# Rotary positions loaded into the table rows and the tables computed there; value stores issued by ScalarE

## The chip, the cores and the metric

The kernel runs on one core of a Trainium2 chip. The metric is the device time of one execution in microseconds (us). The engines are TensorE (PE; its weight loads are a row of their own, PEld), VectorE (DVE), ScalarE (ACT), GpSimd (POOL) and SyncE (SP), which here only issues transfers (DMAs). Each engine works through its own instructions strictly in order and waits on semaphores for what others produce.

## What is computed

One decoder layer on a sequence of 2048 tokens, model width 1024, float32. Cut to what matters here:

```python
mod = silu(c) @ w_ada + b_ada;  shift, scale, gate = split(mod, 3)
h = rms_norm(x, norm_pre) * (1 + scale) + shift
xa, ga, q, k, v, gb = split(h @ w_in)             # six groups of 512 columns
ang = positions[:, None] * 10000 ** (-arange(32) / 32)
cos, sin = cos(ang), sin(ang)                     # one table for all 8 heads
q, k = rotary(q, cos, sin), rotary(k, cos, sin)   # x1*cos - x2*sin, x2*cos + x1*sin
ya = rms_norm(rg_lru(conv(xa)) * silu(ga))
yb = rms_norm(dilated_attention(q, k, v) * silu(gb))
out = x + gate * rms_norm(concat(ya, yb) @ w_out, norm_post)
```

## The kernel before, in words

The first phase (to about 650 us of the span) makes h and all projections; attention follows, then the output projection. The change touches the first phase alone.

The sequence is cut into four chunks c of 512 tokens, done in two halves (chunks 0 and 1, then 2 and 3). Float32 products are split in high and low parts, three matmuls each. In a half the order of the program is: q and k of the first four heads for both chunks (`qk`, L376), recurrent blocks (`rec`, which calls `conv`, `ga`, `lru`), q and k of the other heads, more recurrent blocks, the values (`v`, L398) and the gate of attention (`gb`, L408). `load(c)` (L1007) loads a chunk of x, normalises it, and for chunks 2 and 3 makes the rotary table; `prep(c)` transposes it on PE (L298) and makes the high and low parts of h, `hh` on ACT (L308) and `hl` on DVE or POOL (L311, L313). In the first half `prep(1)` stands behind q and k of chunk 0, `load(2)` behind the k of the second four heads, `prep(2)` and `load(3)` behind the gate of chunk 0. The table of chunk 0 (`trig(0)`) is called ahead of `prep_h` of chunk 0, that of chunk 1 just ahead of `prep(1)`.

`trig(c)` (L238) takes a scratch buffer from `turn()`, which hands out two buffers, `half_t` and `rot_t`, in turn. The same two are the workspace of every `qk` and, in the first half, of `gb`; each is stored to DRAM from there. `trig` loads the 512 positions of the chunk to all 128 partitions of the scratch buffer (L243), converts them to float, multiplies by the frequencies, takes off multiples of two pi (DVE, L245 to L251), takes two sines and an absolute value on ACT (L253 to L256), and writes cosine and sine to rows of `cos_t` (DVE, L258 to L260). `cos_t` has four rows of 512: cosine and sine of even chunks, then of odd chunks.

`v` evacuates each tile of values from PSUM on ACT (L404) into `vr`, of which there are two buffers, and stores it to DRAM through SP's queue (L406). SP's queue also carries the weight loads (`wst`, three buffers that the loads of the gate's weights, `wgate`, L206, share; L327), the loads of x (L269) and the stores of q, k, y and gb (L395, L501, L420).

The order of instructions in this phase is not written by hand. A planner orders the instructions of each engine, and the transfers of each queue, by the order of the program and its own estimates of durations; work whose inputs it expects to be ready goes into idle time ahead of work that comes earlier in the program. On the chip this order is then fixed. The attention phase has its order written out by hand.

The DMAs that SP issues are not ordered by data alone: SP issues them one after the other, and an issue that waits holds all behind it.

Of the kernel before, what the change touches and what calls it, by code (L numbers as in the profile page):

```python
# [9 lines left out]
I32 = mybir.dt.int32  # L10
AF = mybir.ActivationFunctionType
ALU = mybir.AluOpType
# [4 lines left out]
P = 128  # L17
# [5 lines left out]
CH = 512  # L23
# [27 lines left out]
INV_TWO_PI = 1.0 / (2.0 * math.pi)  # L51
MAGIC = 12582912.0


class Layer:
# [179 lines left out]
        return self.turns[0]  # L235


    def trig(self, c):  # L238
        nc = self.nc
        v = nc.vector  # L240
        rot = self.turn()
        pi = rot[:, 0, :].bitcast(I32)
        nc.sync.dma_start(pi, self.io["positions"][:, c * CH:(c + 1) * CH].to_broadcast([P, CH]))  # L243
        a = rot[:, 1, :]
        v.tensor_copy(a, pi)  # L245
        v.tensor_scalar(a, a, self.freq, None, ALU.mult)
        n = rot[:, 2, :]
        v.tensor_scalar(n, a, INV_TWO_PI, MAGIC, ALU.mult, ALU.add)
        v.tensor_scalar(n, n, MAGIC, None, ALU.subtract)
        for part in (TWO_PI_1, TWO_PI_2, TWO_PI_3):  # L250
            v.scalar_tensor_tensor(a, n, -part, a, ALU.mult, ALU.add)  # L251
        s = rot[:, 2, :]
        nc.scalar.activation(s, a, AF.Sin, scale=0.5)  # L253
        nc.scalar.activation(a, a, AF.Abs)
        ch = rot[:, 3, :]
        nc.scalar.activation(ch, a, AF.Sin, scale=-0.5, bias=self.halfpi)  # L256
        cos, sin = (self.cos_t[:, 2 * (c % 2) + n, :] for n in range(2))
        v.tensor_mul(cos, s, s)  # L258
        v.tensor_scalar(cos, cos, -2.0, 1.0, ALU.mult, ALU.add)
        v.scalar_tensor_tensor(sin, s, 2.0, ch, ALU.mult, ALU.mult)  # L260
        return cos, sin


# [134 lines left out]
    def v(self, rw, ps, h, w, quad, c):  # L398

        nc = self.nc  # L400
        for t in range(4):
            o = self.tmajor(ps, w, h, t, "pv")
            vr = rw.tile([P, 4, DH], F32, name="vr", bufs=2)
            nc.scalar.activation(vr, o[:, 0:256].rearrange("p (h d) -> p h d", d=DH), AF.Copy, scale=0.5)  # L404
            r0 = c * CH + t * P
            nc.sync.dma_start(self.v_s[r0:r0 + P, 4 * quad:4 * quad + 4, :], vr)  # L406

    def gb(self, wst, ps, h, w, half, c):  # L408

# [547 lines left out]
    def run(self, out):  # L957
        tc, nc = self.tc, self.nc
        self.wst_bufs = 3
        with ExitStack() as top:  # L960
            def pool(stack, name, bufs=1, **kw):
                return stack.enter_context(tc.tile_pool(name=name, bufs=bufs, **kw))
# [30 lines left out]
            with ExitStack() as p1:  # L993
                psx = pool(p1, "psx", space=PSUM)
                rw = pool(p1, "rw")
                wpb = pool(p1, "wpb")
                recb = pool(p1, "recb")
                h0p = pool(p1, "h0p")
                ps = Banks((psm, 2), (psx, 4))
                hs, self.cs = {}, {}  # L1000

                def slot(c):
                    return (h1p, "s1") if c % 2 else (h0p, "s0")

                xs = {}

                def load(c):  # L1007
                    xs[c] = self.load_x(c)
                    self.normalise(rw, ps, xs[c], first=c < 2)
                    if c > 1:  # L1010
                        self.cs[c] = self.trig(c)

                def prep(c):
                    hs[c] = self.prep_h(*slot(c), c, lambda k: self.transpose_x(ps, xs[c], k), c == 1)

                with tc.tile_pool(name="ld", bufs=1) as ld:
                    x0 = []
                    self.constants(const, ld, ps, lambda: x0.extend(self.load_x(0)))
                    self.normalise(rw, ps, x0, first=True)
                    raw = []  # L1020
                    for k in range(KC):
                        rp, tag = (recb, ("xr", "xc", "xh", "xl", "ga", "a", "m")[k]) if k < 7 else (reca, "xc")
                        raw.append(rp.tile([P, CH], F32, name=f"raw{k}", tag=tag))
                        pt = self.transpose_x(ps, x0, k)
                        nc.scalar.copy(raw[k], pt)
                    ws = [h1p.tile([P, 4, 2, 512], F32, name="wada", tag=t) for t in ("s1h", "s1l")]
                    self.ada_half(ws, reca, "ri", ps, ld, 0)
                    wq = self.weights(wpa, wst, OQ, rotary=True, early=True)
                    self.ada_half(ws, recb, "ri", ps, ld, 1)
                    wk = self.weights(wpb, wst, OK_, rotary=True, early=True)  # L1030
                    self.cs[0] = self.trig(0)
                    hs[0] = self.prep_h(*slot(0), 0, lambda k: raw[k], True)
                    load(1)
                    self.gate_steps = self.ada_gate(wst, ps, ld)
                    for half in range(2):
                        c0, c1 = 2 * half, 2 * half + 1

                        def rec(j):
                            w = self.weights(wpa, wst, OXA + P * j, col2=OGA + P * j)
                            us = []  # L1040
                            for c, rp in ((c0, reca), (c1, recb)):
                                us.append(self.conv(rp, ps, hs[c], w, 0, j, c))
                                self.ga(ps, hs[c], w, 1, us[-1])
                            self.defer(3, lambda: self.lru(ps, us))

                        def values(q):
                            w = self.weights(wpb, wst, OV + 256 * q)
                            for c in (c0, c1):
                                self.v(rw, ps, hs[c], w, q, c)

                        if half:
                            wq = self.weights(wpa, wst, OQ, rotary=True)
                            wk = self.weights(wpb, wst, OK_, rotary=True)
                        for c in (c0, c1):
                            self.qk(ps, hs[c], wq, "q", 0, c)
                            self.qk(ps, hs[c], wk, "k", 0, c)
                            if c == c0:
                                if c1 == 1:
                                    self.cs[1] = self.trig(1)
                                prep(c1)  # L1060
                        if half == 0:
                            self.softplus(ld)
                            self.gate_weights(gwp, reca)
                        rec(0)
                        w = self.weights(wpb, wst, OQ + 256, rotary=True)
                        for c in (c0, c1):
                            self.qk(ps, hs[c], w, "q", 1, c)
                        rec(1)
                        w = self.weights(wpb, wst, OK_ + 256, rotary=True)
                        for c in (c0, c1):  # L1070
                            self.qk(ps, hs[c], w, "k", 1, c)
                        if half == 0:
                            load(2)
                        rec(2)
                        values(0)
                        rec(3)
                        values(1)
                        wb = [self.weights(wp, wst, OGB + 256 * q) for q, wp in enumerate((wpa, wpb))]
                        for c in (c0, c1):
                            for q in range(2):  # L1080
                                self.gb(wst, ps, hs[c], wb[q], q, c)
                            if c == 0:
                                prep(2)
                                load(3)
                    whole(self.gate_steps)
                    self.tick(6)
# [74 lines left out]
def whole(steps):  # L1161

    while True:
        try:
            next(steps)
        except StopIteration as e:
            return e.value
# [67 lines left out]
```

## Time and profile before

| | before |
|---|---|
| median of three runs | 1184.37 us (1180.71 to 1185.92) |
| the profiled execution | 1180.56 us, its span 1178.8 us |
| PE busy | 1096.3 us (93%) |
| DVE busy | 758.4 us (64%) |
| ACT busy | 612.6 us (52%) |
| POOL busy | 457.3 us (39%) |
| mean granted TensorE clock | 0.965 of full speed |

The page also cuts the span in 40 slices of 29.5 us; each digit is the busy share of a slice in tenths (9 is 90% or more), PEclk the granted clock:

```profile
PE   5868999869989999999999999999999998999996
DVE  4766497677555645879565266687597783355556
ACT  5544353447547223654545377767678674223332
PEclk9988999999999999999999999989999989999998
```

The first phase is the first 22 slices. PE is below 9 in slices 0, 1, 2 and 3, in slice 8 (236 to 265 us) and in slice 11 (324 to 354 us).

### The profile page before, as it was taken

The numbers are of one execution on the slowest core, as the hardware profiler recorded it, in microseconds if no ns is written. First come the engines' busy times: TensorE is split into PE (matmuls) and PEld (weight loads), VectorE is DVE, ScalarE is ACT, GpSimd is POOL, SyncE is SP. The second block draws the span as 40 slices with busy tenths as digits, with TensorE's granted clock in tenths as the row PEclk, the third lists the DMA queues.
The fourth block names the chain that finished last, engine by engine and source line by source line (L and its number), as shares of the span: only waits on it lengthen the run. The fifth ranks groups of instructions, "written<-read, shape, count | busy, mean of one in ns | idle before, by whom it ended". The sixth has DMA issues, their size and how long they took to land.

```text
span 1178.8 us, 18472 instructions
## 1 busy us (share of the span) xinstructions
PE 1096.3 (93%) x6645; PEld 899.0 (76%) x6645; DVE 758.4 (64%) x1655; ACT 612.6 (52%) x1512; POOL 457.3 (39%) x297
## 2 busy tenths in 40 slices
PE   5868999869989999999999999999999998999996
PEld 2546888768967778888898888878777876778885
DVE  4766497677555645879565266687597783355556
ACT  5544353447547223654545377767678674223332
POOL 1434434234143553436234170083361563742222
PEclk9988999999999999999999999989999989999998
DMA  9533335152253344427222724858659447976654
GB/s 338 191 116 131 116 119 169 60 180 90 85 147 125 110 141 135 124 91 196 82 90 77 227 77 98 179 135 221 164 124 236 127 146 147 269 231 215 186 152 143
DMA packets 164859, 176.49 MB, mean 150 GB/s; under 512 B 25168, under 2 KB 119840, under 8 KB 164768
## 3 DMA queue, kind: packets, MB, share of 16 engines
q1 hardware_dynamic: 164768, 175.32, 51.9%
q8 instruction: 52, 0.85, 0.3%
q14 instruction: 39, 0.32, 0.1%
HBM read 124.49 MB, written 50.79 MB: 149 GB/s over the span
## 4 chain that ended last, share of the span: by engine, by line
PE 52%; DMA 18%; DVE 12%; POOL 7%; issue 5%; ACT 4%; SPq 2%; DVEq 0%; POOLq 0%; ACTq 0%
PE sp L665 5%; DMA st_s<-stat 3%; PE pt L688 3%; DMA wgate<-in_w_ada 3%; DMA W<-f_s 2%; PE pvo L705 2%; PE pv L369 2%; PE pv L370 2%; PE pv L371 2%; PE pmixa L909 2%; POOL W L805 2%; PE pmixb L927 2%; PE pmixa L907 2%; PE pgb L358 2%; PE pgb L357 2%
## 5 line engine op out<-in xcount | busy, mean ns | idle before, releaser
L344 POOL TENSOR_TENSOR wl<-wst,wh 128x1024 fp32r<-128x1024 f32 (+2 forms) x72 | 138.5, 1945 | 203.1 <-ACT wh L342 203.1
L670 DVE CUSTOM_DVE_ANT_0 pm<-sp,table 128x256 f32<-128x256 f32 (+1 forms) x384 | 119.2, 360 | 48.3 <-PE sp L665 42.9
L665 PE MATMUL sp<-kh,qs 64*128 64x256 f32 (+1 forms) x768 | 131.9, 388 | 8.9 <-DVE S L670 5.2
L805 POOL TENSOR_TENSOR W<-W,o 128x512 f32<-128x512 f32 x48 | 60.7, 1294 | 151.0 <-DMA W<-f_s 151.0
L665 PEld LDWEIGHTS sp<-kh,qs 64*128 64x128 f32 x768 | 100.8, 274 | 24.0 <-issue 12.4
L688 PE MATMUL pt<-table,pm 128*128 128x128 f32 x600 | 88.8, 294 | 2.7 <-ACT pT L693 1.5
L705 PE MATMUL pvo<-pT,vt 128*64 128x128 f32 (+1 forms) x1072 | 87.6, 306 | 0.0
L342 ACT CAST wh<-wst 128x1024 fp32r<-128x1024 f32 (+2 forms) x72 | 51.8, 761 | 56.3 <-DMA wst<-in_w_in 26.6
L688 PEld LDWEIGHTS pt<-table,pm 128*128 128x128 f32 x600 | 69.4, 148 | 15.1 <-issue 3.0
L369 PE MATMUL pv<-wh,hh 128*128 128x256 f32 x256 | 72.8, 284 | 7.6 <-ACT vr L404 4.4
L705 PEld LDWEIGHTS pvo<-pT,vt 128*64 128x64 f32 x1072 | 63.4, 144 | 19.2 <-issue 14.4
L370 PE MATMUL pv<-wl,hh 128*128 128x256 f32 x256 | 72.7, 284 | 3.6 <-POOL wl L344 3.6
L952 POOL TENSOR_TENSOR mix<-mix,xt 128x1024 f32<-128x1024 f32 x15 | 36.6, 2441 | 100.1 <-DVE mix L951 60.1
L665 PE MATMUL sp<-kl,qs 64*128 64x256 f32 (+1 forms) x384 | 75.4, 366 | 0.0
L678 ACT ACTIVATE pm<-pm,stat 128x256 f32<-128x256 f32 (+1 forms) x128 | 60.2, 474 | 25.5 <-DVE stat L670 25.5
L371 PE MATMUL pv<-wh,hl 128*128 128x256 f32 x256 | 72.3, 282 | 0.0
L678 ACT ACTIVATE pm<-pm,turn 128x256 f32<-128x256 f32 (+1 forms) x128 | 62.8, 495 | 16.3 <-DVE turn L670 16.3
L357 PE MATMUL pa<-hl,wh 128*128 128x512 f32 x128 | 52.7, 412 | 17.0 <-DVE hl L313 14.7
L691 DVE COPY pT<-pt 128x512 f32<-128x512 f32 (+1 forms) x96 | 63.7, 679 | 0.8 <-PE pt L688 0.5
L665 PEld LDWEIGHTS sp<-kl,qs 64*128 64x128 f32 x384 | 57.8, 277 | 0.0
L437 DVE SCALAR_TENSOR_TENSOR xc<-xr,cols,xc 128x512 f32<-128x512 f32 x48 | 55.5, 1156 | 0.8
L369 PEld LDWEIGHTS pv<-wh,hh 128*128 128x128 f32 x256 | 49.0, 191 | 8.8 <-ACT vr L404 5.1
(275 smaller groups left out, 3131.8 us busy)
## 6 DMA issues: line engine op xcount, KB each, us to landing
wst<-in_w_in SPq DMA_DIRECT2D x32, 512.0 KB
W<-f_s SPq DMA_DIRECT2D x32, 384.0 KB
x_t<-in_x SPq DMA_DIRECT2D x16, 512.0 KB
wada<-in_w_ada SPq DMA_DIRECT2D x16, 512.0 KB
wst<-in_w_in SPq DMA_DIRECT2D x32, 256.0 KB
vt<-v_s SPq DMA_DIRECT2D x32, 256.0 KB
yat<-y_s SPq DMA_DIRECT2D x32, 256.0 KB
yb_s<-yb SPq DMA_DIRECT2D x16, 512.0 KB
```

The lines of the kernel that those rows point to most:

```text
L344: nc.gpsimd.tensor_tensor(lo, i, hi.bitcast(F32), ALU.subtract)
L357: nc.tensor.matmul(o, lhsT=wh[:, k, sl], rhs=hl[:, k, :], start=False, stop=False)
L369: nc.tensor.matmul(o[:, 0:256], lhsT=hh[:, k, sl], rhs=wh[:, k, :], start=k == 0, stop=False)
L370: nc.tensor.matmul(o[:, 0:256], lhsT=hh[:, k, sl], rhs=wl[:, k, :], start=False, stop=False)
L371: nc.tensor.matmul(o[:, 0:256], lhsT=hl[:, k, sl], rhs=wh[:, k, :], start=False, stop=k == KC - 1)
L665: nc.tensor.matmul(self.sp[h][:, o:o + n], lhsT=x[rows, q], rhs=y[rows, k], start=j == 0, stop=j == 2)
L670: v.tensor_tensor_reduce(out=pm[:, o:o + n], in0=sp[:, o:o + n], in1=self.mask[:, 256 - n:256], scale=-0.125, scalar=3e38, op0=ALU.add, op ...
L678: nc.scalar.activation(pm[:, o:o + n], pm[:, o:o + n], AF.Exp, bias=self.stat(ctx, s, b), scale=-1.0, accum_out=self.stat(ctx, 2 + s, b))
L688: nc.tensor.transpose(pt[:, k * P:(k + 1) * P], pm[:, k * P:(k + 1) * P], self.ident)
L691: nc.vector.tensor_copy(pT[:, 0:tot], pt[:, 0:tot])
L705: self.mark = nc.tensor.matmul(self.bank[p][64 * s:64 * s + 64, o:o + w], lhsT=ctx["vt"][p, b][:, s], rhs=ctx["pT"][:, c:c + w], start=fir ...
L805: e.tensor_tensor(W[:, p], W[:, p], self.o.pop((pr, p, n)), ALU.mult)
```

## The change

Positions no longer go through a scratch buffer. A new method loads them straight into the sine row of the chunk in `cos_t`; for chunks 0 and 1 it is called ahead of the modulation (`ada_half`), for chunks 2 and 3 where `load(c)` called `trig`. `trig` takes no turn of the two buffers: its steps run in place in the two rows of `cos_t`. It has the same number of instructions on DVE (ten) and on ACT (three); the product for the sine now comes before the two steps that turn the half-angle sine into the cosine. As `trig` takes no turn, the buffers of all later `qk` and `gb` calls alternate by themselves. In `v`, the store is issued on ACT's queue.

```diff
+    def load_positions(self, c):
+        pi = self.cos_t[:, 2 * (c % 2) + 1, :].bitcast(I32)
+        self.nc.sync.dma_start(pi, self.io["positions"][:, c * CH:(c + 1) * CH].to_broadcast([P, CH]))
+
     def trig(self, c):
...
-        rot = self.turn()
-        pi = rot[:, 0, :].bitcast(I32)
-        nc.sync.dma_start(pi, self.io["positions"][:, c * CH:(c + 1) * CH].to_broadcast([P, CH]))
-        a = rot[:, 1, :]
-        v.tensor_copy(a, pi)
...
+        cos, sin = (self.cos_t[:, 2 * (c % 2) + n, :] for n in range(2))
+        v.tensor_copy(sin, sin.bitcast(I32))
+        v.tensor_scalar(sin, sin, self.freq, None, ALU.mult)
+        v.tensor_scalar(cos, sin, INV_TWO_PI, MAGIC, ALU.mult, ALU.add)
+        v.tensor_scalar(cos, cos, MAGIC, None, ALU.subtract)
         for part in (TWO_PI_1, TWO_PI_2, TWO_PI_3):
-            v.scalar_tensor_tensor(a, n, -part, a, ALU.mult, ALU.add)
...
+            v.scalar_tensor_tensor(sin, cos, -part, sin, ALU.mult, ALU.add)
+        nc.scalar.activation(cos, sin, AF.Sin, scale=0.5)
+        nc.scalar.activation(sin, sin, AF.Abs)
+        nc.scalar.activation(sin, sin, AF.Sin, scale=-0.5, bias=self.halfpi)
+        v.scalar_tensor_tensor(sin, cos, 2.0, sin, ALU.mult, ALU.mult)
+        v.tensor_mul(cos, cos, cos)
         v.tensor_scalar(cos, cos, -2.0, 1.0, ALU.mult, ALU.add)
-        v.scalar_tensor_tensor(sin, s, 2.0, ch, ALU.mult, ALU.mult)
...
     def v(self, rw, ps, h, w, quad, c):
...
-            nc.sync.dma_start(self.v_s[r0:r0 + P, 4 * quad:4 * quad + 4, :], vr)
+            nc.scalar.dma_start(self.v_s[r0:r0 + P, 4 * quad:4 * quad + 4, :], vr)
...
                 def load(c):
...
                     if c > 1:
+                        self.load_positions(c)
+                    if c > 1:
                         self.cs[c] = self.trig(c)
...
                     ws = [h1p.tile([P, 4, 2, 512], F32, name="wada", tag=t) for t in ("s1h", "s1l")]
+                    for c in range(2):
+                        self.load_positions(c)
                     self.ada_half(ws, reca, "ri", ps, ld, 0)
```

## Rows read from the trace of the kernel before

**Rows 1.** By stretch: busy PE, PEld, DVE, ACT, POOL (instructions), granted clock, DMA share, GB/s.
```profile
0.00:25.00 25.00, 12.38 (x40) 4.50 (x41) 13.46 (x49) 13.97 (x26) 0.19 (x4) 1.00 0.94 331
50.00:80.00 30.00, 23.24 (x96) 17.07 (x96) 27.39 (x42) 18.45 (x32) 11.36 (x9) 0.89 0.28 83
80.00:110.00 30.00, 18.26 (x76) 14.60 (x75) 14.02 (x24) 10.18 (x19) 9.12 (x5) 0.77 0.31 114
210.00:260.00 50.00, 41.53 (x245) 35.98 (x245) 38.31 (x47) 24.28 (x37) 19.87 (x10) 0.99 0.37 119
260.00:300.00 40.00, 35.62 (x189) 30.91 (x188) 29.10 (x31) 24.37 (x39) 16.14 (x8) 0.88 0.31 100
335.00:365.00 30.00, 22.83 (x117) 18.60 (x116) 18.24 (x27) 16.53 (x23) 7.18 (x6) 0.89 0.34 97
400.00:450.00 50.00, 47.40 (x218) 37.82 (x217) 25.42 (x32) 16.41 (x25) 25.11 (x16) 1.00 0.41 120
560.00:640.00 80.00, 80.00 (x502) 72.01 (x501) 47.87 (x50) 46.48 (x76) 30.26 (x14) 1.00 0.25 84
```

**Rows 2.** Waits, 60 to 120 us: total us, times, longest.
```profile
DVE half_t L245 <- DMA half_t<-in_positions: 12.2, 1, 12.2
PE pa L357 <- DVE hl L313: 12.2, 2, 11.7
```

**Rows 3.** Timeline of DVE: start us, duration us, instruction, idle before it.
```profile
93.07 0.43 DVE L245 CAST half_t<-half_t 128x512 f32<-128x512 int32 x1 [12.21 <-DMA half_t<-in_positions]
93.41 0.69 DVE L313 TENSOR_TENSOR hl<-x_t,hh 128x512 fp32r<-128x512 f32 x1
```

**Rows 4.** Timeline of SP's queue, 70 to 84 us.
```profile
74.24 7.31 SPq L395 DMA_DIRECT2D k_s<-rot_t  x3
81.66 2.34 SPq L243 DMA_DIRECT2D half_t<-in_positions  x1
```

**Rows 5.** Busy time by stretch, just behind that wait.
```profile
96.00:99.00 3.00, 3.00 (x10) 2.41 (x9) 2.45 (x5) 1.44 (x2) 1.66 (x1) 0.50 0.00 0
```

**Rows 6.** DVE by line, 48 to 64 us: busy us, mean ns, idle before.
```profile
L251 DVE SCALAR_TENSOR_TENSOR rot_t<-rot_t 128x512 f32<-128x512 f32 x3 | 2.0, 678 | 0.0
L259 DVE TENSOR_SCALAR cos_t<-cos_t 128x512 f32<-128x512 f32 x1 | 1.4, 1406 | 0.0
```

**Rows 7.** Waits of PE, 48 to 80 us.
```profile
PE xT L298 <- DVE x_t L311: 3.4, 1, 3.4
```

**Rows 8.** Waits of all engines, 200 to 225 us.
```profile
POOL half_t L387 <- DVE half_t L385: 19.9, 1, 19.9
DVE rot_t L245 <- DMA rot_t<-in_positions: 10.8, 1, 10.8
```

**Rows 9.** Waits of PE, 225 to 260 us.
```profile
PE pv L370 <- POOL wl L344: 3.6, 2, 2.5
PE pv L369 <- ACT xc L435: 3.3, 1, 3.3
```

**Rows 10.** Timeline of ACT, 250 to 266 us, and of SP's queue, 246 to 262 us.
```profile
265.43 0.71 ACT L404 ACTIVATE vr<-pv 128x256 f32<-128x256 f32 x2 [6.08 <-DMA v_s<-vr]
...
260.94 0.38 SPq L327 DMA_DIRECT2D wst<-in_w_in  x1
261.41 0.56 SPq L406 DMA_DIRECT2D v_s<-vr  x1
```

**Rows 11.** Waits of all engines, 335 to 358 us.
```profile
PE xT L298 <- DVE x_t L311: 6.4, 1, 6.4
DVE half_t L245 <- DMA half_t<-in_positions: 3.9, 1, 3.9
```

**Rows 12.** The line of the value stores; waits of SP's queue, 0 to 655 us.
```profile
L406 SPq DMA_DIRECT2D v_s<-vr x32: 319/320/564, 252.3 to 625.6; - x32
...
SPq L406 <- DMA wst<-in_w_in: 3.0, 1, 3.0
```

**Rows 13.** DVE by line, 4 to 17 us.
```profile
L134 DVE TENSOR_SCALAR spacc<-spacc 128x4 f32<-128x4 f32 x7 | 1.2, 170 | 0.2
```

More of the change, by code (lines that the diff above doesn't have):

```diff
@@ L240, in trig @@
         v = nc.vector
-        rot = self.turn()
-        pi = rot[:, 0, :].bitcast(I32)
-        nc.sync.dma_start(pi, self.io["positions"][:, c * CH:(c + 1) * CH].to_broadcast([P, CH]))
-        a = rot[:, 1, :]
-        v.tensor_copy(a, pi)
[L246 to L249, printed above, removed]
-        for part in (TWO_PI_1, TWO_PI_2, TWO_PI_3):
-            v.scalar_tensor_tensor(a, n, -part, a, ALU.mult, ALU.add)
[L252 to L258, printed above, removed]
+        cos, sin = (self.cos_t[:, 2 * (c % 2) + n, :] for n in range(2))
[3 more added lines that the diff above has]
+        v.tensor_scalar(cos, cos, MAGIC, None, ALU.subtract)
+        for part in (TWO_PI_1, TWO_PI_2, TWO_PI_3):
+            v.scalar_tensor_tensor(sin, cos, -part, sin, ALU.mult, ALU.add)
[4 more added lines that the diff above has]
+        v.tensor_mul(cos, cos, cos)
         v.tensor_scalar(cos, cos, -2.0, 1.0, ALU.mult, ALU.add)
-        v.scalar_tensor_tensor(sin, s, 2.0, ch, ALU.mult, ALU.mult)
         return cos, sin
```

## The prediction, made before the changed kernel was run

> **What bounds the kernel now.** I read the busy shares first: PE is the fullest engine, and the changed lines all lie in the first phase, so the question is where PE stands idle there and who holds it. The busy time by stretch answers the first half [rows 1]: PE has no gap in long stretches such as 560 to 640 us, and loses its time in few places: 50 to 80 us (30 - 23.24 = 6.8 us idle), 80 to 110 (11.7), 210 to 260 (8.5), 260 to 300 (4.4) and 335 to 365 (7.2), 38.6 us in all. Each but the third also drags the granted clock down, to a mean of 0.77 to 0.89; behind the longest wait PE is fully busy at a granted clock of 0.50, the lower of its two levels (1.2 of 2.4 GHz) [rows 5]. Then the waits say who held it. In all five places a line of the change is in it.
>
> The largest place shows the pattern. SP issues the positions of chunk 1 at 81.66 us, behind the four stores of k [rows 4]; they land 11.4 us later, since DVE's first step of the table starts at 93.07 [rows 3]. DVE waits 12.2 us for them, PE 11.7 us [rows 2], though PE needs nothing of that table yet: it needs `hl`, and L313 stands behind L245 in DVE's order and starts as soon as L245 is through [rows 3]. So the loss is not the work of the table but the place of a waiting instruction in an in-order queue.
>
> **The change part by part.** All sums are against the profiled execution, 1180.56 us (span 1178.8 and 1.8 around it).
>
> *Chunk 1 (80 to 110 us).* The load moves from 81.66 us to the front of SP's queue, so L245 has nothing to wait for wherever the planner puts it. That takes 11.7 us off PE [rows 2], and the low clock with it: a mean of 0.77 over 30 us is 0.23 / 0.5 x 30 = 13.8 us at the lower level, of which about 9 fell in the idle time and 5 were work at half speed, 2.5 us lost. Next in line is `prep(1)` itself: DVE still has three pairs of L311 and L313 to do, at 0.7 to 0.8 us each, and PE may wait for the last; I keep 1.7 us for that. Gain 12.5 us, between 8 and 14.
>
> *The table of chunk 0 (50 to 80 us).* DVE is busy 27.4 of 30 us here [rows 1], and the chain of waits runs through it. Ten instructions of the table, 0.4 to 1.4 us each (the three of L251 make 2.0 us, L259 1.4 [rows 6]), are 7.1 us of it. With positions there from the start they can run in DVE's idle time before 50 us (25 - 13.46 = 11.5 us in the first 25 [rows 1]). That the planner does such things is seen: the softplus steps, which the program calls behind q and k of chunk 0, ran among the first instructions, at 4 to 17 us [rows 13]. PE would have x of chunk 1 earlier, on which it waits 3.4 us [rows 7] of its 6.8, with another 1.7 us at the lower clock (0.11 / 0.5 x 30 = 6.6 us, about half of it work). The new order of the sine and cosine products makes the cosine wait for one ACT step and one product more, about 1.5 us, which is hidden if the table is early. Bounds: -4 (the moved steps get in the way further up) and +8.5; I take +4.5, the middle, nearest to the wait of 3.4 us and its clock.
>
> *The start.* Two loads of 0.26 MB now stand ahead of the modulation's weights, in a stretch with a DMA share of 0.94 at 331 GB/s [rows 1]: 0.52 MB / 331 GB/s = 1.6 us later for the weights. Chunk 0's load was already in the busy stretch, and PE has slack of under a microsecond there: -1 us, between 0 and -1.6, plus what the moved DVE steps cost (above).
>
> *Chunk 2 (210 to 260 us).* DVE waits 10.8 us for positions, POOL 19.9 us for DVE behind that [rows 8], and PE then waits 3.6 us for POOL's `wl` and 3.3 for ACT's `xc`, both late from that [rows 9]: 6.9 us. The load no longer waits for the stores of the scratch buffer, but for DVE's last reading of the sine row, a few microseconds earlier, and is issued ahead of the stores of k rather than behind. The landing itself stays, so I leave DVE 3 of its 10.8 us, and PE 3 / 10.8 of its loss, 1.9 us. Gain 5, between 0 and 7.
>
> *The value stores (255 to 275 us).* ACT waits 6.1 us to reuse `vr` [rows 10]: the store of its last content was issued only at 261.41, behind a weight load that SP had waited to issue till 260.94. PE waits 4.4 us of the 4.4 idle in 260 to 300, and 5 us of work there ran at the lower clock (0.12 / 0.5 x 40 = 9.6 us, less 4.4 idle), 2.6 us. On ACT's queue the store is issued as soon as the tile is written. The price is 32 issues of 0.32 us [rows 12], 10.2 us of ACT; in the second half they lie beside a PE that is full while ACT is busy 46 of 80 us [rows 1], so they cost nothing there, and in the first half ACT has 15.6 of 40 us free. If that cover were gone, all 10.2 us would count. Gain 6 of 7, between -3 and 7.
>
> A rule speaks against this part. The Trainium skill (DMA: Bandwidth & Descriptors, "Issuing engines are not separate DMA queues") says that transfers from any issuing engine share the same 16 DMA engines, and that issuing from several only saves issue time. By that rule 0.32 us per store would be all, and the sum would end 6 us later. The trace differs in what an issue can cost: here SP's queue held a store behind another transfer's wait, and ACT's reader for 6.1 us [rows 10].
>
> *Chunk 3 (335 to 365 us).* DVE waits 3.9 us for positions, which waited for a store of gb out of `half_t`, and PE 6.4 us behind it [rows 11]; 0.11 / 0.5 x 30 = 6.6 us at the lower clock, half of it work, 1.6 us lost. The sine row of chunk 1 is free 100 us earlier, so the table can be made long before. Of 7.2 + 1.6 us I take 7.5, between 4 and 9. Of ACT's table loads I expect as many as before, since the three activations stay.
>
> *What stays.* Stretches without such a wait keep small ones (2.6 us in 400 to 450 [rows 1]); the new order will have its own. I take off 3 us. Attention and the output projection start earlier by the sum and do not change.
>
> Sum: 12.5 + 4.5 - 1 + 5 + 6 + 7.5 - 3 = 31.5 us. 1180.6 - 31.5 = 1149.1 in the profiled execution. The median of the runs is 3.8 us above it, so I predict 1153 us.
>
> **The rivals.**
>
> *Positions still late.* The loads of chunks 2 and 3 may land behind stores of k again, as in rows 4, with DVE's L245 placed too early by a planner whose estimate was wrong by 10 us before. For: rows 8 show that error. Against: the sine row is free before the stores are ready. Then chunk 2 gives nothing and chunk 3 half: 1153 + 5 + 3.5 = 1161.5, say 1162. 18%.
>
> *The moved tables get in the way.* Two tables of 7.1 us are 14.2 us of DVE against 11.5 us idle in the first 25, and the modulation that all waits for runs on DVE there. Then 50 to 80 us loses 4 instead of gaining 4.5: 1153 + 8.5 = 1161.5. 12%.
>
> *The store's move saves SP's issue time only.* That is so if ACT's 6.1 us were the flight of the store and not its place in the queue; of the 6.1, 4.0 lie behind the issue at 261.41 [rows 10]. PE off its path, the 0.32 us per issue [rows 12] are worth nothing: 1153 + 6 = 1159. 8%. This is the case in which the skill's rule above holds in full.
>
> *ACT is held at the store (the other side).* SP's value store once waited 3.0 us for a weight load that has nothing to do with it [rows 12]; if an issue has to wait for the end of an earlier, unrelated transfer, ACT waits with it, and behind it stand the recurrence's activations and the next evacuations. In 260 to 300 and 560 to 640 us, where 19 of the 32 stores lie by their times, ACT is free for 15.6 and 33.5 us [rows 1], 2.6 us per store. With a hold of 4.0 us each (the time from a store's issue to its reader [rows 10]) it would be 1.4 us too late per store, 32 x 1.4 = 45 us; less the 25.5 us of the other parts that is 19 us slower than before: 1203. It outweighs the gains from 2.6 + 25.5 / 32 = 3.4 us per store on. One such wait in 32 speaks against it. 5%.
>
> *The change does nothing to the waits* (the planner puts the steps where they were and other waits take their place): 1184. 5%.
>
> **How the numbers follow.** Forecast 52%, rivals 18, 12, 8, 5 and 5. About 0.5% (6 us) is what a measurement can tell from no change. The forecast and the first three rivals lie 22 us or more below the median: 0.90 together, of which I take 0.04 off, half to each side, for a mix of losses that the cases don't name: faster 0.86, same 0.05 + 0.02 = 0.07, slower 0.05 + 0.02 = 0.07. Low end: all 38.6 us of idle time and 8.4 of clock back would be 1137 (with the 3.8); I take 1138. High end: chunk 1 alone, 1180.6 - 12.5 + 3.8 = 1172. That leaves out the last two rivals and some 8% of the rest.
>
> **What would show it.** Right: no wait of DVE for positions at chunk 1, PE without a gap at 80 to 95 us, no stall of ACT at L404, the page's slices 8 and 11 at 9, the clock near 1.0 from 80 to 365 us, and q and k of the second half starting about 30 us earlier. Wrong: L245 still behind a landing, waits of ACT at L406, PE starting later than before in the first 30 us, or a longer attention phase.

## The result and the profile after

The changed kernel takes 1167.1 us in the median (1165.3 to 1168.4), the one before 1183.5 beside it: a ratio of 0.9861, interval 0.9833 to 0.9890. That is 16.4 us, about half of the 31.5 us that I had summed. The time lies in the range of 1138 to 1172, 14 us above the 1153 that I forecast.

The page of the changed kernel: its span is 1164.1 us (1165.9 with what lies around it), PE is busy 1093.3 us, the granted clock is 0.970. Busy tenths in 40 slices of 29.1 us:

```profile
PE   4879999889999999999999999999999998999996
PEclk9989999989999999999999899989999988999999
```

PE's slices 8 and 11, 6 and 8 before, are 8 and 9 now; slice 7, at 8 before too though I had not listed it, stays at 8; slice 0 has fallen from 5 to 4. So something was gained in the middle and something lost at the front. The stretches of [rows 1] (and one more, 25 to 50 us) show how much; the columns are those of there:

```profile
0.00:25.00 25.00, 10.16 (x29) 4.03 (x30) 15.61 (x53) 15.43 (x27) 0.19 (x4) 1.00 0.93 323
25.00:50.00 25.00, 20.13 (x77) 8.80 (x76) 22.53 (x35) 11.60 (x25) 11.93 (x12) 1.00 0.86 307
50.00:80.00 30.00, 24.90 (x104) 17.08 (x101) 15.65 (x28) 15.00 (x29) 11.86 (x11) 0.90 0.26 74
80.00:110.00 30.00, 26.52 (x115) 21.07 (x116) 22.62 (x31) 13.95 (x29) 14.82 (x9) 0.88 0.41 141
210.00:260.00 50.00, 43.46 (x256) 38.80 (x255) 41.78 (x50) 33.42 (x49) 20.21 (x10) 0.90 0.39 124
260.00:300.00 40.00, 40.00 (x251) 36.11 (x251) 31.72 (x33) 22.96 (x38) 16.96 (x8) 1.00 0.40 126
335.00:365.00 30.00, 30.00 (x146) 24.24 (x145) 13.97 (x20) 18.94 (x37) 12.45 (x9) 1.00 0.43 147
```

Two stretches came out as forecast: 260 to 300 and 335 to 365 us have PE full at a clock of 1.00. In 80 to 110 us PE still lacks 3.5 us and in 210 to 260 us 6.5 us, at clocks of 0.88 and 0.90, where I had expected nearly 1.0, and in 25 to 50 us, where it had 23.4 us of work before, 4.9 us.

A stretch of the clock compares other work once the kernels have drifted apart, so I set three milestones beside them: the first weight load of the first recurrent block (pxa), of the attention gate (pgb) and of the scores (sp). Line, instruction, count, three durations, first and last start. Before:

```profile
L356 PEld LDWEIGHTS pxa<-hh,wh x128: 187/188/188, 114.5 to 589.9; 128*128 128x128 f32 x128
L356 PEld LDWEIGHTS pgb<-hh,wh x128: 187/188/333, 321.8 to 666.7; 128*128 128x128 f32 x128
L665 PEld LDWEIGHTS sp<-kh,qs x768: 182/307/333, 667.7 to 970.8; 64*128 64x128 f32 x192
```

After:

```profile
L355 PEld LDWEIGHTS pxa<-hh,wh x128: 186/188/189, 110.1 to 571.5; 128*128 128x128 f32 x128
L355 PEld LDWEIGHTS pgb<-hh,wh x128: 187/188/193, 312.2 to 648.3; 128*128 128x128 f32 x128
L664 PEld LDWEIGHTS sp<-kh,qs x768: 182/307/333, 649.4 to 955.9; 64*128 64x128 f32 x192
```

The differences: 4.4 us gained to the first pxa, 5.2 more to the first pgb (207.3 became 202.1), 8.7 more to the first score (345.9 became 337.2), 18.3 in all. From there to the end of the span it is 514.7 us instead of 511.1, so 3.6 are gone again.

**The front.** The last small matmuls of the modulation (L191), before and after:

```profile
47.10 1.05 PE L191 MATMUL adac<-ones,half_t 1*128 1x1 f32 x8
...
54.74 1.05 PE L191 MATMUL adac<-ones,half_t 1*128 1x1 f32 x8
```

They are 7.6 us late. DVE's timeline of the changed kernel shows by what (start, duration, instruction, idle before it):

```profile
13.04 0.42 DVE L248 CAST cos_t<-cos_t 128x512 f32<-128x512 int32 x1
...
17.98 0.68 DVE L253 SCALAR_TENSOR_TENSOR cos_t<-cos_t 128x512 f32<-128x512 f32 x1
18.58 0.75 DVE L177 TENSOR_SCALAR acc<-wada,silu_c 128x1024 f32<-128x1024 f32 x1
19.24 1.28 DVE L253 SCALAR_TENSOR_TENSOR cos_t<-cos_t 128x512 f32<-128x512 f32 x2
20.45 1.27 DVE L179 SCALAR_TENSOR_TENSOR acc<-wada,silu_c,acc 128x1024 f32<-128x1024 f32 x1
```

All twenty steps of two tables stand between 13 and 34 us, among the sums of the modulation (L177, L179), which everything waits for. They also push other work back. The small steps of the softplus, at 4 to 17 us before [rows 13], now stand in part among the sums of the modulation's second half, which ran without a break before (from 37.06 to 43.36 us). DVE after:

```profile
41.13 1.76 DVE L179 SCALAR_TENSOR_TENSOR acc<-wada,silu_c,acc 128x1024 f32<-128x1024 f32 x1
42.81 0.68 DVE L133 TENSOR_TENSOR spacc<-spacc,sps 128x4 f32<-128x4 f32 x1
...
45.45 3.92 DVE L179 SCALAR_TENSOR_TENSOR acc<-wada,silu_c,acc 128x1024 f32<-128x1024 f32 x3
```

PE's matmuls on the finished sums (L183) start 2.6 us late in the first half (28.97 us, 26.34 before) and 6.0 us late in the second (49.42, 43.42 before).

**Chunk 1.** DVE no longer waits for positions. The waits of 60 to 120 us have other names instead (total, times, longest):

```profile
DVE w_rg_x_h L155 <- DMA w_rg_x_st<-in_w_rg_x: 7.5, 1, 7.5
PE xT L297 <- DVE x_t L310: 6.4, 1, 6.4
```

A weight of the recurrence, wanted by the first recurrent block from 110 us on, is now the load behind which DVE stands, and PE behind DVE: the figure of [rows 2 to 4] with another load.

**Chunk 2.** PE waits as long as in [rows 9], 225 to 262 us:

```profile
PE pv L369 <- POOL wl L343: 3.4, 1, 3.4
PE pv L368 <- ACT wh L341: 3.2, 1, 3.2
```

although DVE's wait for positions there is 0.4 us instead of 10.8:

```profile
DVE cos_t L248 <- DMA cos_t<-in_positions: 0.4, 1, 0.4
```

**Value stores.** ACT's waits to reuse `vr` from 245 to 655 us before, and PE's wait behind them; then ACT's waits after:

```profile
ACT vr L404 <- DMA v_s<-vr: 24.1, 6, 8.5
PE pv L369 <- ACT vr L404: 4.4, 1, 4.4
...
ACT vr L403 <- DMA v_s<-vr: 7.6, 5, 4.7
```

### The profile page after: what moved, and what is told of

Its sections match the earlier page's. It is cut to its first block, busy times and chain, and to the rows that moved or that the text cites. A ratio compares the mean times of both kernels' runs of the same rounds, so it can differ in the third digit from the quotient of the medians.

```text
span 1164.1 us, 18452 instructions
## 1 busy us (share of the span) xinstructions
PE 1093.3 (94%) x6645; PEld 896.5 (77%) x6645; DVE 760.8 (65%) x1655; ACT 611.1 (52%) x1511; POOL 453.3 (39%) x297
## 4 chain that ended last, share of the span: by engine, by line
PE 59%; DMA 12%; DVE 12%; POOL 6%; ACT 5%; issue 4%; SPq 2%; DVEq 0%; POOLq 0%; ACTq 0%
PE sp L664 5%; PE pt L687 3%; PE pvo L704 3%; PE pv L369 3%; DMA st_s<-stat 3%; PE pv L370 3%; PE pv L368 3%; PE pgb L357 3%; PE pgb L355 3%; PE pgb L356 3%; DMA wgate<-in_w_ada 2%; PE pmixb L926 2%; PE pmixb L927 2%; PE pmixb L928 2%; PE pmixa L908 2%
## 5 line engine op out<-in xcount | busy, mean ns | idle before, releaser
L951 POOL TENSOR_TENSOR mix<-mix,xt 128x1024 f32<-128x1024 f32 x15 | 36.6, 2443 | 98.7 <-DVE mix L950 45.3
L436 DVE SCALAR_TENSOR_TENSOR xc<-xr,cols,xc 128x512 f32<-128x512 f32 x48 | 56.1, 1168 | 1.0 <-ACT xc L434 0.2
L906 PE MATMUL pmixa<-wo,yat 128*128 128x512 f32 x128 | 51.5, 403 | 5.3 <-DMA yat<-y_s 5.3
```

## The experiments

Each ratio is to the kernel before, timed on the same chip; that one's median moved between 1183.5 and 1187.1 us from chip to chip, so ratios are compared and not medians. "Front" is the start of the last L191, "late part" runs from the first score to the end of the span. All times in us, from the profiles; the interval is of the ratio. A profile is one execution: those of positions only, three edits and value weights first are 6.3, 6.5 and 8.8 us faster than the median of their kernel, so that ratios decide on the total and the columns only on where time goes.

| kernel | ratio (interval) | front | first pxa | first pgb | first sp | late part |
|---|---|---|---|---|---|---|
| before | 1 | 47.1 | 114.5 | 321.8 | 667.7 | 511.1 |
| changed | 0.9861 (0.9833 to 0.9890) | 54.7 | 110.1 | 312.2 | 649.4 | 514.7 |
| changed, again | 0.9832 (0.9804 to 0.9860) | 55.3 | 112.4 | 316.7 | 653.8 | 510.4 |
| stores only | 0.9928 (0.9901 to 0.9955) | 45.8 | 113.7 | 314.5 | 658.4 | 514.9 |
| positions only | 0.9928 (0.9896 to 0.9961) | 54.7 | 110.0 | 320.7 | 657.8 | 510.8 |
| late positions | 0.9816 (0.9785 to 0.9847) | 47.7 | 105.7 | 308.1 | 645.2 | 519.1 |
| gate stage | 0.9823 (0.9788 to 0.9859) | 53.9 | 101.6 | 307.1 | 644.2 | 517.1 |
| early load, late table | 0.9836 (0.9807 to 0.9865) | 48.0 | 105.5 | 309.2 | 648.1 | 520.1 |
| last table late | 0.9844 (0.9816 to 0.9871) | 53.9 | 109.3 | 312.0 | 650.8 | 518.4 |
| three edits | 0.9827 (0.9792 to 0.9862) | 45.7 | 104.8 | 306.4 | 645.2 | 514.6 |
| value weights first | 0.9921 (0.9894 to 0.9948) | 54.7 | 111.6 | 321.0 | 658.1 | 508.5 |
| late, stage, values | 0.9878 (0.9836 to 0.9920) | 47.8 | 107.0 | 314.7 | 651.8 | 517.5 |
| gate piece later | 0.9866 (0.9838 to 0.9894) | 53.0 | 109.8 | 312.7 | 651.2 | 515.2 |
| all, gate later | 0.9830 (0.9788 to 0.9872) | 45.3 | 103.0 | 306.8 | 645.3 | 517.1 |

**Stores only.** The kernel before, with the one line of the value stores.

```diff
-            nc.sync.dma_start(self.v_s[r0:r0 + P, 4 * quad:4 * quad + 4, :], vr)
+            nc.scalar.dma_start(self.v_s[r0:r0 + P, 4 * quad:4 * quad + 4, :], vr)
```

> Only the value stores go to ScalarE's queue; positions and tables as before the change. Theory (a store held behind SP's other transfers cost PE 4.4 us and 2.6 us of low clock at 255 to 275 us): ACT's waits for v_s stores, 24.1 us before, fall under 6 us, PE stands for none of them, the time falls by 4 to 8 us to about 1177. Rival (issue time only): no change, 1183 +- 2, and PE's 4.4 us stay.

From the first pxa to the first pgb it needs 200.8 us instead of 207.3, and to the first score 2.0 less after that. ACT's waits for the stores in the whole phase:

```profile
ACT vr L404 <- DMA v_s<-vr: 12.3, 5, 4.7
```

24.1 us have become 12.3; I had expected less than 6. PE's wait of 4.4 us is gone, and PE is full from 260 to 300 us (40.00 of 40). One line differs, so the store's place in SP's order was the cost.

**Positions only.** The changed kernel with the value stores back on SP.

```diff
-            nc.scalar.dma_start(self.v_s[r0:r0 + P, 4 * quad:4 * quad + 4, :], vr)
+            nc.sync.dma_start(self.v_s[r0:r0 + P, 4 * quad:4 * quad + 4, :], vr)
```

> Positions and tables as in the changed kernel, value stores on SP's queue. Theory: the changed kernel's time plus what the stores give, 1172 to 1175, with ACT again 10 us or more behind v_s stores. Rival (the stores gave nothing): 1167.

The first pxa is that of the changed kernel, 110.0 us; from there to the first pgb it needs 210.7 us, 3.4 longer than before; from there to the first score 337.1, 8.8 shorter. The positions pay at chunks 1 and 3 and not at chunk 2. With the stores on SP, ACT waits 25.4 us for them again, and PE behind it (225 to 300 us):

```profile
PE pv L368 <- ACT vr L403: 4.6, 1, 4.6
```

The two halves of the change, each 0.0072, add up to 0.0144, against 0.0139 for both.

**Late positions.** The changed kernel; chunks 0 and 1 load their positions behind the modulation.

```diff
-                    for c in range(2):
-                        self.load_positions(c)
                     self.ada_half(ws, reca, "ri", ps, ld, 0)
...
+                    for c in range(2):
+                        self.load_positions(c)
                     self.cs[0] = self.trig(0)
```

> The changed kernel, but the positions of chunks 0 and 1 are loaded behind the modulation's weights, so that neither loads nor table steps can stand in front of the modulation. Theory (the early tables on DVE delay the modulation): its last small matmuls (L191) end at 48 us as before the change, not at 55.5; the two tables then lie in 50 to 75 us again, so that only part of the 7 us is kept: 1161 to 1166. Rival (the delay is not from the tables): L191 ends at 54 us or later, 1167 or more.

The front is back at 47.7 us, the first pxa 4.4 us earlier than in the changed kernel. But what is taken out of the front lands behind it (stretches 25 to 50 and 50 to 80 us):

```profile
25.00:50.00 25.00, 23.39 (x93) 11.94 (x93) 15.08 (x23) 10.94 (x26) 14.06 (x16) 0.97 0.81 292
50.00:80.00 30.00, 21.48 (x83) 15.49 (x82) 29.83 (x50) 19.99 (x35) 11.24 (x9) 0.84 0.28 79
```

DVE is full from 50 to 80 us, and PE has 21.5 us of work there instead of 24.9. The median, 1163.4 us, is as I expected.

**Gate stage.** The changed kernel; the staging tiles of the recurrence's gate weights lie in two buffers that are free from the start.

```diff
-            st = ld.tile([P, 4, P], F32, name=nm + "_st", tag="xc")
+            st = ld.tile([P, 4, P], F32, name=nm + "_st", tag="ga" if nm == "w_rg_a" else "m")
```

> The changed kernel, but the two gate weights of the recurrence get a staging buffer each that is free from the start, so that their loads don't wait for a slot. Theory (DVE's conversion of w_rg_x, waiting 7.5 us for its load at 72 us, took the place of the wait for positions): DVE waits under 1 us there, PE's wait of 6.4 us for L310 goes with its low clock, 1158 to 1161. Rival (prep of chunk 1 is held by q and k of chunk 0 anyway): another wait of 4 us or more in 70 to 90 us, 1165 to 1168.

DVE's wait at L155 is gone, PE's wait for `xT` falls from 6.4 to 0.4 us, and the first pxa comes 8.5 us earlier. Of these, 5.1 are left at the first pgb: PE's two waits at the first values are again 3.4 and 3.2 us, and three of 1.1 to 1.4 us stand ahead of them. DVE has another wait in its place, 8.2 us up to 116.24 us for a piece of the output gate (L214), but this time PE does not stand behind it. The median, 1163.5 us, lies between my two cases.

**The changed kernel again.**

> The changed kernel once more, as the base for the three kernels beside it on one chip, and to see how steady the part behind the first phase is. Theory: the attention phase and the output projection took 514.7 us in the changed kernel's profile against 511.1 us before, and between 510.8 and 519.1 us in the other kernels, whose code there is the same; if that is scatter of an execution, this profile shows another value between 510 and 520 us, with the first score product at 649 to 650 us as before. Rival: the change makes that part 3.6 us longer; then it is again within 0.5 us of 514.7 us. The ratio to the kernel before should be 0.985 to 0.989 by either.

The late part took 510.4 us, against 514.7 in the first profile of the same kernel, and 508.5 to 520.1 over all kernels with the same code there. So the 3.6 us that I had to explain are within what one execution differs from another; its first pxa is 2.3 us later than in the first profile, and from there to the first pgb it needs 204.3 us instead of 202.1. I had expected the first score at 649 to 650 us and a ratio of 0.985 to 0.989; 653.8 us and 0.9832 miss both. A single profile can't tell differences of 2 us in one part, nor of 4 us in the total.

**Early load, late table.** The changed kernel; the second step of the tables of chunks 0 and 1 also reads, times zero, a column of the modulation, so that the tables can't be made before it. The loads stay in front.

```diff
+    def freq_of(self, c):
+        if c > 1:
+            return self.freq
+        self.nc.vector.scalar_tensor_tensor(self.freq2, self.G[:, 4:5], 0.0, self.freq, ALU.mult, ALU.add)
+        return self.freq2
...
-        v.tensor_scalar(sin, sin, self.freq, None, ALU.mult)
+        v.tensor_scalar(sin, sin, self.freq_of(c), None, ALU.mult)
```

> The changed kernel, with the positions of chunks 0 and 1 loaded at the front as in it, but the second step of these two tables multiplies by a copy of the frequencies that also reads (times zero) a column of the gate, so that VectorE cannot make the tables among the steps of the modulation. One instruction of 128x1 more per table. Theory (the 20 table steps in VectorE's order delayed the modulation): its last small matmuls end at 47 to 50 us, as in the kernel before (47.9), against 55.5 us in the changed kernel, and the total is within 3 us of that with the late loads (ratio 0.980 to 0.984). Rival (the 0.52 MB in front of the modulation's weights delayed it): they end at 54 to 56 us again, and the total stays at 0.985 to 0.989.

The front ends at 47.95 us, 0.9 us later than before and 6.8 earlier than in the changed kernel, so the steps of the tables made it late, and not the loads. The ratio, 0.9836, is at the upper end of what I expected (0.980 to 0.984) and no better than the changed kernel's beside it (0.9832): the tables fill DVE from 50 to 80 us as with the late positions (29.86 of 30 us).

**Last table late.** The changed kernel; chunk 3's table waits, by the same means, for the last state of the recurrence.

```diff
+        self.nc.vector.scalar_tensor_tensor(self.freq2, self.hlast[2], 0.0, self.freq, ALU.mult, ALU.add)
```

> The changed kernel, with the second step of chunk 3's table reading (times zero) the last state of the recurrence that is made late in the half, so that this table cannot be hoisted to 217 to 244 us. Theory (that table, ten steps of VectorE and the loads of ScalarE's activation tables around its sines, takes back what chunk 2's early positions gave): the two waits of TensorE there, 3.4 us for wl and 3.2 us for wh, shrink to under 2 us together, the first score product comes 4 to 6 us earlier than 649.4 us, total 1160 to 1163 us. Rival (chunk 2's own table and the order of the recurrence there hold TensorE): the waits stay at 5 to 7 us and the total is within 2 us of the changed kernel; chunk 3's table may then even cost 2 to 4 us where it goes.

A miss. The table went away from 217 to 244 us, and the waits stayed (200 to 262 us):

```profile
PE pv L377 <- POOL wl L351: 3.0, 1, 3.0
PE pv L376 <- ACT wh L349: 2.4, 1, 2.4
```

My theory that the early table of chunk 3 gives back chunk 2's gain falls.

**Three edits together** (late positions, gate stage, last table late).

> The changed kernel with three edits together: positions of chunks 0 and 1 loaded behind the modulation, the staging tiles of the gate's weights in buffers that are free from the start, and chunk 3's table made late. Theory (three separate losses that do not overlap): first score product 4.2 (late positions) + 5.2 (staging) + 4 to 6 (last table) us earlier than 649.4 us, 634 to 638 us, total 1151 to 1156 us, ratio to the kernel before about 0.973 to 0.977. Rival (the waits replace each other, as before): the total is no better than the best single edit, 1160 to 1164 us.

Also a miss: the single gains at the first pxa don't add (104.8 us), and the ratio is that of the single edits. From the first pxa to the first pgb it needs 201.6 us, as the changed kernel does (202.1).

**Value weights first.** POOL's timeline of the changed kernel shows what `wl` stands behind:

```profile
224.74 1.55 POOL L498 TENSOR_TENSOR yl<-ri,yh 128x512 fp32r<-128x512 f32 x1 [2.54 <-ACT yh L497]
226.25 1.81 POOL L504 TENSOR_TENSOR ysq<-ysq,ri 128x512 f32<-128x512 f32 x1
229.94 1.67 POOL L498 TENSOR_TENSOR yl<-ri,yh 128x512 fp32r<-128x512 f32 x1 [1.88 <-ACT yh L497]
231.57 1.45 POOL L504 TENSOR_TENSOR ysq<-ysq,ri 128x512 f32<-128x512 f32 x1
232.99 5.64 POOL L343 TENSOR_TENSOR wl<-wst,wh 128x1024 fp32r<-128x1024 f32 x2
```

In the kernel before the same split stood ahead of those four steps:

```profile
230.34 6.04 POOL L344 TENSOR_TENSOR wl<-wst,wh 128x1024 fp32r<-128x1024 f32 x2
```

Counted from the first pxa, `wl` now starts 122.9 us after it instead of 115.8. So I called the weights of the first values earlier in the program:

```diff
+                        w = self.weights(wpb, wst, OV) if half == 0 else None
                         if half == 0:
                             load(2)
                         rec(2)
-                        values(0)
+                        values(0, w)
```

> The changed kernel, with the weights of the first values called (loaded and split) ahead of the third recurrent block in the first half instead of behind it. In the order of GpSimd the two wl splits of 128x1024 then stand ahead of the two yl and ysq pairs of the recurrence instead of behind them, in that of ScalarE the two wh splits ahead of yh. Theory (TensorE's 6.6 us there are the place of the split behind the recurrence's tail, as the kernel with the late last table suggests): wl starts at about 222 instead of 233 us, TensorE's waits of 3.4 us for wl and 3.2 us for wh are gone, the stretch from the first pxa to the first pv shrinks from 121.8 to about 117 us, the first score product comes 5 to 8 us earlier (641 to 645 us), total 1159 to 1162 us. Rival (VectorE, busy 33 of 35 us from 215 to 250 us, is the bound there): the recurrence's tail is late by as much, TensorE waits 4 us or more for xh, xl or pxa's evacuation between 225 and 260 us, and the first score product stays at 647 to 651 us.

The waits for `wl` and `wh` are gone, and a longer one has come 30 us ahead of them (100 to 262 us):

```profile
PE pb L355 <- DVE rot_t L385: 10.5, 2, 9.7
```

DVE's timeline of this kernel gives the reason:

```profile
208.83 1.28 DVE L216 SCALAR_TENSOR_TENSOR GP<-wgate,silu_c,GP 128x1024 f32<-128x1024 f32 x1 [9.34 <-DMA wgate<-in_w_ada]
210.03 0.69 DVE L384 TENSOR_TENSOR rot_t<-pb,cos_t 128x512 f32<-128x512 f32 x1
```

Four loads of weights in a row pushed the load of a piece of the output gate (`wgate`) behind them. DVE's step on that piece, wanted hundreds of us later, stands ahead of the two products that free `pb`. It is neither of my two cases: a third load at the head of the same line.

**Late, stage, values** (with the first two edits at the start).

> The changed kernel with three edits together: positions of chunks 0 and 1 behind the modulation, the staging tiles of the gate's weights in free buffers, and the first values' weights ahead of the third recurrent block. Theory (each takes away one wait of its own): first pxa at 100 to 104 us, 117 us from there to the first pv, first score product at 634 to 640 us, total 1148 to 1156 us, ratio to the kernel before 0.970 to 0.977. Rival (between the first pxa and the values another engine is the bound, so that what the start gives is given back there, as in the kernel with the three other edits, whose first pv came only 4.8 us earlier): first pv at 224 to 228 us, first score product at 642 to 646 us, total 1158 to 1164 us.

The same wait, 9.6 us, and a ratio of 0.9878: a miss for the theory.

**Gate piece later.** As value weights first, and that call draws no piece of the gate.

```diff
-        if not early:
+        if gate and not early:
             next(self.gate_steps, None)
...
+                        w = self.weights(wpb, wst, OV, gate=False) if half == 0 else None
```

> The kernel with the values' weights called first, once more, but that call draws no piece of the modulation's gate: in it the load of such a piece (wgate) went to the end of a row of four loads of weights, and VectorE's step for it (GP, L216) waited 9.3 us ahead of the rotary products that free pb, on which TensorE waited 9.7 us. Now no GP step stands ahead of those products. Theory (the row of loads and that one step took back what the earlier split gave): TensorE's wait for pb is under 2 us, those for wl and wh stay away, from the first pxa to the first pv 116 to 119 us, first score product 641 to 646 us, total 1157 to 1163 us, ratio 0.977 to 0.983. Rival (the loads themselves are too late there, three buffers of staging being too few for three sets of weights): TensorE still waits 4 us or more between 190 and 260 us, for weights or for the first table of the second half, first score product 647 us or later, ratio 0.985 or above.

My expectation had a wrong premise: the piece drawn by an earlier call still stands ahead of the products in DVE's order and waits 8.6 us, PE 4.9 us behind it.

```profile
202.14 1.28 DVE L216 SCALAR_TENSOR_TENSOR GP<-wgate,silu_c,GP 128x1024 f32<-128x1024 f32 x1 [8.56 <-DMA wgate<-in_w_ada]
```

PE's waits for `wl` and `wh` are gone here too, and yet from the first pxa to the first pgb it needs 202.9 us, no less than the changed kernel. The first score at 651.2 us and the ratio of 0.9866 are those of my rival.

**All, gate later** (with the two edits at the start).

> The same together with the two edits at the start: positions of chunks 0 and 1 behind the modulation, staging of the recurrence's gate weights in free buffers. Theory (the three losses are separate): first pxa at 101 to 107 us, first pv 116 to 119 us later, first score product 635 to 641 us, total 1150 to 1157 us, ratio 0.971 to 0.977. Rival (what one wait gives, the next takes): first score product 644 us or later, ratio 0.980 or above, as with the other combinations.

First score at 645.3 us, ratio 0.9830: the rival. No version is shown to be faster than the changed kernel: the intervals of all with a lower ratio overlap with that of its second timing.

## Why the prediction was half right

The mechanism held at chunks 1 and 3 and for the stores: engines that work in order stood behind transfers that they did not need yet, and taking a transfer out of the line gave time back. It failed at the start and at chunk 2. That the range held the time does not speak for the sum: its high end was chunk 1 alone, and an excess at chunk 3 that I had not foreseen made up for a part of what the start lost. The terms of the sum, to the first score:

| term | predicted | measured | from |
|---|---|---|---|
| start | -1 | -7.6 | front, 47.1 to 54.7 |
| table of chunk 0 and chunk 1 | +17 | +12.0 | 4.4 to the first pxa, plus 7.6 |
| chunk 2 | +5 | -1.3 | 202.1 against 200.8 of stores only; nothing, within the scatter of 2.2 (with the stores on SP -3.4, 210.7 against 207.3) |
| value stores | +6 | +6.5 | stores only, first pxa to first pgb |
| chunk 3, less the residue | +4.5 | +8.7 | first pgb to first score |
| sum | +31.5 | +18.3 | |

**The start** is the step that failed most, by 6.6 us. "In a stretch with a DMA share of 0.94" I priced the bytes, and these cost little: with the loads in front and the tables late the front is at 47.95 us, and at 45.3 to 47.8 in the six profiles in which those two loads do not stand together in front. With the tables' steps among the sums it is at 53.0 to 55.3, in seven profiles. PE's work of the first 25 us, 10.16 us where it was 12.38, is one of my signs of being wrong. I left the twenty steps of DVE out of the term ("plus what the moved DVE steps cost (above)"; above, they are no more than the low bound of chunk 0's term) and took DVE's 11.5 us of idle time in 0 to 25 us for free space. DVE was idle there between the sums of the modulation, for whose end PE waits; the planner put the table's steps between them, and some of the softplus steps, which I had cited as proof that it uses such gaps, between the later sums. The rival of the tables that get in the way had the mechanism at 12%, but its price in the wrong place: it made 50 to 80 us lose, and there the changed kernel has 24.9 us of PE instead of 23.2. The two single edits that take the steps out give 7.0 and 6.8 us at the front, of which 4.4 and 4.6 are left at the first pxa. The +4.5 for chunk 0's table also was not the middle of its bounds, as I wrote: between -4 and +8.5 that is 2.25.

**Chunk 1.** I wrote that next in line is `prep(1)` and kept 1.7 us. Next in line was another load: of 11.7 us idle PE kept 6.4, for `w_rg_x` (gate stage takes that wait away, and gives 8.5 us at the first pxa). I had looked at what DVE would do next on the path, not at which other loads stand in its order.

**Chunk 2.** I priced the wait by its share (3 of 10.8 us kept); the wait went nearly whole, to 0.4 us, and nothing was gained. What PE needs there is the split of the value weights, and the new order put it behind the recurrence's last steps on POOL and ACT. Four rearrangements left 201.6 to 203.8 us between the first pxa and the first pgb (three edits, last table late, gate piece later, all with gate later), against 202.1, and value weights first and late, stage, values even 209.4 and 207.7: the loss around 200 to 250 us went from one wait to the next. DVE's wait for positions and the place of chunk 3's table are excluded as its cause. What bounds that stretch stays open. The value weights' place was not tried cleanly, since each time a wait for a piece of the gate came with it, and a kernel without both was not run. Nor did a run move chunk 2's own table, whose first sine now stands between two steps of the recurrence on ACT:

```profile
212.39 1.28 ACT L254 ACT_TABLE_LOAD   x1
213.68 0.64 ACT L254 ACTIVATE cos_t<-cos_t 128x512 f32<-128x512 f32 x1
214.34 1.28 ACT L484 ACT_TABLE_LOAD   x1
215.63 0.72 ACT L484 ACTIVATE ri<-ri,c 128x512 f32<-128x512 f32 x1
```

The sine and a load of ACT's function table on either side of it hold the recurrence for 3.2 us, and `yh`, for which POOL waits ahead of `wl`, comes behind it. In the kernel before this sine came later (load at 231.00 us), behind these steps; every profile of a kernel with the changed positions has it between them. ACT loads about as many function tables as before in the whole program (34, 35 before), as I expected, but 7 instead of 3 from 200 to 260 us. What this costs PE is not shown.

**Value stores.** Right: 6.5 us in this stretch (8.5 us by the ratio of stores only), since SP's order no longer held the stores. ACT was not held at its own 32 issues, which took 0.33 to 0.35 us each, so the rival on the other side is excluded. The rule of the Trainium skill (DMA: Bandwidth & Descriptors, "Issuing engines are not separate DMA queues"), by which another issuing engine saves issue time alone, is not the whole price here: stores only shows ACT's waits halved.

**Chunk 3.** Right: PE full, clock 1.00 from 335 to 365 us. Positions only has the whole of it, 8.8 us. The residue of 3 us that I took off did not show in this part.

**After the first phase** I expected no change; 3.6 us more in the profiled run are within the scatter of single executions shown above.

## What to carry to other kernels

When a waiting instruction is taken out of an in-order engine, list every other load that the same engine's next instructions need, and when it will land; the next such load takes over most of the wait. Idle time of an engine between the steps of a chain is not free space: a planner that fills it delays the chain, by the steps themselves and by the work that they push back. Count such a gain at the next milestones too, since half of it may be given back where another order was hidden behind the old wait.

## What the runs showed of the hardware

DVE was slow beside POOL's wide subtractions. In the changed kernel L436 on 128x512 takes 0.75 us with POOL idle, and 2.86 us while POOL works on `wl` (232.99 to 238.63 us, above); DVE's timeline:

```profile
236.31 2.86 DVE L436 SCALAR_TENSOR_TENSOR xc<-xr,cols,xc 128x512 f32<-128x512 f32 x1
...
243.23 0.75 DVE L436 SCALAR_TENSOR_TENSOR xc<-xr,cols,xc 128x512 f32<-128x512 f32 x1
```

The Trainium skill (SBUF — State Buffer, "Who interferes with whom") states that a VectorE instruction with two inputs in SBUF contends with a GpSimd instruction that reads SBUF; these rows agree. Moving the value weights' split earlier on POOL moves this too, which I had not counted: in gate piece later, where `wl` runs from 227.02 to 232.68 us, L253 and L494 on 128x512 take 2.82 and 2.88 us there and 0.68 us behind it. How much of the stretch from 200 to 250 us hangs on it was not tried.
